# Eighteen of 24 gate tiles made ahead of the attention, as nine pairs in seven block products each

## The chip, the cores and the metric

The kernel runs on one core of a Trainium2 chip. The metric is the time of one execution on the device in microseconds; the profile is of one such execution. TensorE (PE) makes the products, and loads its weights in a stream of its own (PEld); VectorE (DVE), ScalarE (ACT) and GpSimd (POOL) do the elementwise work; SyncE (SP) issues most of the transfers.

## What is computed

One layer of a decoder over 1024 tokens of width 1024, all in float32. The normed input u is multiplied by one wide matrix, and the columns of the result go to three mixers and to their gates:

```
u = rmsnorm(x)
[pool_v | q | k | v | f | z | xBC | dt | gates] = u @ W_in
y_A = pooling(pool_v) @ P_pool
y_B = forgetting_attention(q, k, v, f) @ P_attn
y_C = ssd(z, xBC, dt) @ P_ssd
x = x + (sigmoid(g_A)*y_A + sigmoid(g_B)*y_B + sigmoid(g_C)*y_C) @ W_out
x = x + (silu(c_g) * c_v) @ W_down,   [c_g | c_v] = conv3(rmsnorm(x) @ W_up)
out = rmsnorm(x)
```

The gates are 3 x 1024 columns, in the kernel 24 tiles of 128 columns by 1024 tokens.

## The kernel before

A tile of u @ W_in has its 128 columns on the partitions and the 1024 tokens along the row, in two halves of 512. u lies in SBUF for the whole of this part as a high and a low float32r part, `uh` and `ul`, each in two tiles by halves of the tokens, [128, 8, 512] (8 blocks of 128 of the inner dimension). A weight tile is loaded into `wraw` (one buffer) and split into `whi` (ScalarE, L112) and `wlo` (VectorE, L105), three buffers each. `mm3` (L117) makes each product from three: high by high, high by low, low by high (L123). One gate tile is thus 2 halves x 8 blocks x 3 = 48 products of 128x128 by 128x512.

The work comes in this order in the program: the norm and transposes of x; the f and dt columns; the pooling mixer; the SSD mixer in two passes, one for each group g (`ssd_inputs(g)`: six tiles with a convolution, then the z product; `ssd_chunks(g)`: eight chunks of 128 tokens, one after the other through a state); then `gates()`, the first NGATE1 = 8 gate tiles in PSUM tile `big` (2 buffers of two banks), with the sigmoid; then the v product (`in_proj_tok`: 8 token tiles of 24 products each, weights in the three `whi`/`wlo` buffers and a fourth pair, `xhi`/`xlo`). All of this stands in one SBUF pool, `ssd`, whose tiles follow each other in the order in which the program first names them: acc, BT, CT, xs, xhi, xlo, zs, and then those of the chunks, cbm, xd, yt, xdf, xdh, xdl, bth, btl, mt, state and so on. A pool that is opened after another was closed lies on the same addresses, and each of its tiles waits for the tiles of the old one that it lies on.

Then comes the attention (`attend`, four pairs of heads) with `others(pr)` behind each pair: the q and k products of the next pair and some of the other 16 gate tiles, cut by GCUT into 5, 5, 4 and 2. They are made in halves (PSUM tile `half`, L249) and stored without a sigmoid, which `gate_now` applies when it reads them back for the branches. After the attention follow the three branches (`branch4` and the SSD's), the output product, and the FFN.

The order on each engine isn't the program's: when the kernel is built, a scheduler runs through it with a cost model and puts on each engine what is ready by it, first what stands first in the program. So the first gate tiles, and the gates of `others`, are put into the gaps of the SSD chunks and of the attention.

The FFN up product (L1007 to L1083) already works in pairs of tiles with seven block products in place of eight: the 2 x 2 blocks A11 to A22 of a pair of weight tiles, with sums S1 to S4 of them, are multiplied by blocks of the activations (B11, B21, B22) and by sums T1 to T4 of these. Each such product is 4 blocks x 3 = 12 matmuls. `split_next` splits the next operand into a ring of places ahead of its product.

Of the kernel before, what the change touches and what calls it, by code (L numbers as in the profile page):

```python
# [46 lines left out]
def hybrid_kernel(ctx: ExitStack, tc: tile.TileContext, x, xT, w_in, w_z, w_v, w_fd, mixw, p_pool, p_attn,  # L47
# [33 lines left out]
    def bank():  # L81
        return pst("bank")
# [184 lines left out]

    g_d = dpool.tile([24, P, 1024], F32, name="g_d")

    def gate(i, halves):  # L270

        if halves:
            parts = in_proj_halves(T_GATE + i)
        else:
            ps = in_proj(T_GATE + i)
            parts = [(slice(h * 512, (h + 1) * 512), ps[:, h * 512:(h + 1) * 512]) for h in range(2)]
        for hs, ps in parts:
            gt = gpool.tile([P, 512], F32, name="gt")
            if i < NGATE1:
                nc.scalar.activation(gt, ps, AF.Sigmoid)  # L280
            else:
                nc.scalar.copy(gt, ps)
            nc.sync.dma_start(g_d[i][:, hs], gt)
# [157 lines left out]
    NGATE1 = 8  # L441
    GCUT = (0, 5, 10, 14, 16)
    v_d = dpool.tile([NATT, P, NT, 256], F32, name="v_d")
    yn_d = dpool.tile([NT, P, 1024], F32, name="yn_d")
    with ExitStack() as st:
# [130 lines left out]
        def gates():  # L576
            for i in range(NGATE1):
                gate(i, False)
                yield

# [4 lines left out]
        run(gates())  # L585

        for t, ps in in_proj_tok([w_v[kp, 0] for kp in range(4)], sp):
            vs = sp.tile([P, 8, 2, 64], R32, name="vs", tag="xs", bufs=5)
            pv = ps.rearrange("p (h d) -> p h d", d=64)
            nc.scalar.copy(vs[:, :, 0, :], pv)  # L590
            sub_lo(nc.vector, vs[:, :, 1, :], pv, vs[:, :, 0, :])
            nc.sync.dma_start(v_d[:, :, t, :].rearrange("r p c -> p r c"),
                              vs.bitcast(F32).rearrange("p (r h) x d -> p r (h x d)", h=2))
# [36 lines left out]
    with ExitStack() as st:  # L630
# [120 lines left out]
        def others(pr):  # L751

            todo = range(NGATE1 + GCUT[pr], NGATE1 + GCUT[pr + 1])
            res = None
            if pr + 1 < NATT:
                res = yield from qkv(pr + 1)
            for i in todo:
                gate(i, True)
                yield
            return res  # L760
# [83 lines left out]
    def hl(t):  # L844
        return t[:, 0], t[:, 1]

    HL = [P, 2, 4, 512]
    LO, HI = slice(0, 512), slice(512, 1024)
    B11, B21, B22 = [hl(slot(i, HL, R32, n)) for i, n in enumerate(("b11", "b21", "b22"))]

    with ExitStack() as st:
# [77 lines left out]
        def up_load(n):  # L929

            if n < FT:
                q = 2 * ((n + 1) % 2)
                for x in range(2):
                    nc.sync.dma_start(ab[:, q + x, :], f_up[2 * ORDER[n] + x])

        for j in range(5):
            w = load_w(w_out[j])
            if j == 1:
                for i in range(2):
                    nc.sync.dma_start(ab[:, i, :], f_up[2 * i])  # L940
                up_load(0)
            for h in range(2):
                run(out_tile(j, h, w))
# [12 lines left out]

# [3 lines left out]
        LATE, ALL = ("S1", "S2", "S4", "S3"), ("A11", "S1", "S2", "A12", "S4", "S3")  # L960
        ring, parts = [], {}
        todo = []
        for n in range(FT + 1):
            names = [(n, name) for name in (() if n == FT else LATE if ORDER[n] < NPRE else ALL)]
            if n > 0:
                names.insert(names.index((n, "S2")) if names else 0, (n - 1, "A22"))
            todo += names
        n_split = [0]
        s12, s34 = None, ss

        def up_block(n, name):
            if name[0] == "S":
                t, c = (s12, s34)[(int(name[1]) - 1) // 2], (LO, HI)[(int(name[1]) - 1) % 2]
                return t[:, c]
            return ab[:, 2 * ((n + 1) % 2) + int(name[1]) - 1, (LO, HI)[int(name[2]) - 1]]

        SUMS = {"S1": ("A21", "A22", ALU.add), "S2": ("S1", "A11", ALU.subtract), "S3": ("A11", "A21", ALU.subtract),
                "S4": ("A12", "S2", ALU.subtract)}

        def up_sum(n, *names):  # L980

            if n < FT:
                for name in names:
                    x, y, op = SUMS[name]
                    nc.vector.tensor_tensor(up_block(n, name), up_block(n, x), up_block(n, y), op=op)

        def split_next():

            if n_split[0] == len(todo):
                return  # L990
            n, name = todo[n_split[0]]
            hi, lo = ring[n_split[0] % len(ring)]
            n_split[0] += 1
            src = up_block(n, name)
            nc.scalar.copy(hi, src)
            sub_lo(nc.vector, lo, src, hi)
            parts[n, name] = hi, lo
            if name == "A22":
                up_load(n + 2)
            if name == "S2":  # L1000
                if n == 0:
                    up_load(1)
                up_sum(n + 1, "S1", "S2")
            if name == "S3":
                up_sum(n + 1, "S4", "S3")

        def prod(ps, n, name, b, first=True):  # L1007

            w = parts[n, name]
            for k in range(4):  # L1010
                c = slice(k * P, (k + 1) * P)
                m = mm3([ps], (w[0][:, c], w[1][:, c]), [(b[0][:, k, :], b[1][:, k, :])], first and k == 0, k == 3,
                        skip_group_check=not first)
            split_next()
            return m

        def conv_act(i, ca, cb):

            v, g = [sp.tile([P, 1024], F32, name="vg", bufs=2) for _ in range(2)]
            for t, c, acc in ((2 * i + 1, cb, v), (2 * i, ca, g)):  # L1020
                w = [vec[:, V_FW + 3 * t + k:V_FW + 3 * t + k + 1] for k in range(3)]
                nc.scalar.activation(acc, c, AF.Identity, bias=vec[:, V_FB + t:V_FB + t + 1], scale=w[2])  # L1022
                for s in (1, 2):
                    nc.vector.scalar_tensor_tensor(out=acc[:, s:], in0=c[:, 0:1024 - s], scalar=w[2 - s],  # L1024
                                                   in1=acc[:, s:], op0=ALU.mult, op1=ALU.add)
            nc.scalar.activation(g, g, AF.Silu)
            nc.vector.tensor_tensor(g, g, v, op=ALU.mult)
            nc.sync.dma_start(act_d[i], g)
# [21 lines left out]
        def pair(n, c, last):  # L1050


            i = ORDER[n]
            ca, cb = c
            chain, b5 = bank(), bank()
            if i < NPRE:
                for x, t in ((0, cb[:, LO]), (1, ca[:, LO])):
                    nc.sync.dma_start(t, pre_d[i, x])
            else:
                prod(chain, n, "A11", B11)  # L1060
                nc.scalar.copy(ca[:, LO], chain)
            prod(b5, n, "S1", T1)
            nc.scalar.copy(cb[:, HI], b5)
            if last is not None:
                fourth(n - 1, *last)
            prod(chain, n, "S2", T2, first=i < NPRE)
            if i < NPRE:
                nc.tensor.matmul(chain, lhsT=ident, rhs=cb[:, LO], start=False, stop=True, skip_group_check=True)  # L1068
            nc.scalar.copy(ca[:, HI], chain)
            if i >= NPRE:  # L1070
                b2 = bank()
                prod(b2, n, "A12", B21)
                nc.vector.tensor_tensor(ca[:, LO], ca[:, LO], b2, op=ALU.add)
            prod(b5, n, "S4", B22, first=False)
            nc.vector.tensor_tensor(ca[:, HI], ca[:, HI], b5, op=ALU.add)
            prod(chain, n, "S3", T3, first=False)
            nc.vector.tensor_tensor(cb[:, HI], cb[:, HI], chain, op=ALU.add)
            return chain, c

        def fourth(n, chain, c):  # L1080
            prod(chain, n, "A22", T4, first=False)
            nc.scalar.copy(c[1][:, LO], chain)
            conv_act(ORDER[n], *c)  # L1083

# [4 lines left out]
        for i in range(NPRE + 1):  # L1089
# [14 lines left out]
            if i == 2:  # L1104
                s12 = wpool.tile([P, 1024], F32, name="wraw", bufs=WRAW)
                up_sum(0, "S1", "S2", "S4", "S3")
# [4 lines left out]
        for _ in range(3):  # L1111
            hi, lo = [wpool.tile([P, 1024], R32, name=n, bufs=WHL) for n in ("whi", "wlo")]
            ring += [(hi[:, c], lo[:, c]) for c in (LO, HI)]
        ring += [(more[:, 0, r, :], more[:, 1, r, :]) for r in range(4)]
        for _ in range(len(ring)):
            split_next()
        last = None
        for i in range(FT):
            last = pair(i, (cc[:, 2 * (i % 2)], cc[:, 2 * (i % 2) + 1]), last)
# [208 lines left out]
```

## Time and profile before

| | |
|---|---|
| median of 3 runs | 1877.65 us (1876.23 to 1878.08) |
| the profiled execution | 1876.14 us, span 1874.4 us |
| granted TensorE clock, mean | 0.995 |
| busy: PE, DVE, ACT, POOL | 98%, 58%, 46%, 8% of the span |

The page of the profile gives the busy time of each engine, the span in 40 equal slices (a digit is the busy share of a slice in tenths), the chain of waits that ended last, the costliest groups of instructions and the transfers. The time of a single matmul in it includes its pipeline overlap with the next; the distance of starts is what TensorE needs for one.

### The profile page before, as it was taken

What the parts mean: (1) busy time and instruction counts of PE and PEld (TensorE: products, weight loads), DVE (VectorE), ACT (ScalarE), POOL (GpSimd) and SP (SyncE); (2) the same over time, 40 slices, a digit from 0 to 9 for tenths busy, and PEclk for the clock granted to TensorE, in tenths of its full rate; (3) what the DMA queues carried; (4) which work ended last, traced back from release to release, by engine and by line L of the source; (5) the groups of instructions that cost most, each with busy time, mean ns of one, the idle gap of its engine ahead of it and who ended that gap; (6) DMA issues with size and microseconds to landing.
All of it is one profiled execution on the core that took longest, in us unless ns stands there. A gap on an engine that the chain in (4) does not pass through costs nothing.

```text
span 1874.4 us, 22365 instructions
## 1 busy us (share of the span) xinstructions
PE 1841.7 (98%) x8622; PEld 1504.7 (80%) x8622; DVE 1086.6 (58%) x1611; ACT 856.8 (46%) x1384; POOL 157.1 (8%) x119
## 2 busy tenths in 40 slices
PE   7999999999999999999999999999999999999997
PEld 6888888888878778787788888878888888888886
DVE  6752682661265553655765432878787887743424
ACT  5343584573255463654633322545454555533221
POOL 0100240330000000000022002320000000000000
PEclk9999999999999999999999999999999999999998
DMA  4231231333511313124364451443333321664532
GB/s 153 84 120 34 85 108 57 101 130 104 175 65 62 107 51 129 40 90 153 121 200 135 145 180 68 152 135 124 102 107 118 104 91 53 214 235 157 180 102 68
DMA packets 81629, 217.35 MB, mean 116 GB/s; under 512 B 8625, under 2 KB 15217, under 8 KB 80754
## 3 DMA queue, kind: packets, MB, share of 16 engines
q1 hardware_dynamic: 76192, 201.82, 31.9%
q0 software_dynamic: 1728, 8.39, 1.4%
q10 hardware_dynamic: 3602, 5.72, 0.9%
q8 instruction: 67, 1.10, 0.2%
q14 instruction: 40, 0.33, 0.1%
HBM read 164.41 MB, written 51.48 MB: 115 GB/s over the span
## 4 chain that ended last, share of the span: by engine, by line
PE 93%; DVE 2%; DMA 2%; ACT 1%; issue 1%; POOL 0%; SPq 0%; DVEq 0%; ACTq 0%; POOLq 0%
PE p_bank L123 40%; PE p_big L123 19%; PE p_half L123 17%; PE p_bank L265 2%; PE p_bank L264 2%; PE p_bank L263 2%; PE p_po L722 2%; PE p_sc L674 2%; PE p_pt L697 2%; PE p_bank L557 1%; PE p_sc L673 1%; PE p_bank L1068 0%; DMA yi<-yn_d 0%; PE p_bank L324 0%; DMA ab<-in_f_up_dram 0%
## 5 line engine op out<-in xcount | busy, mean ns | idle before, releaser
L105 DVE TENSOR_TENSOR wlo<-wraw,whi 128x1024 fp32r<-128x1024 f32 (+1 forms) x109 | 126.3, 1159 | 162.8 <-ACT whi L112 161.3
L123 PE MATMUL p_bank<-act,whi 128*128 128x512 f32 (+1 forms) x736 | 218.5, 381 | 0.0
L123 PE MATMUL p_big<-uh,whi 128*128 128x512 f32 (+1 forms) x416 | 157.4, 379 | 0.5 <-ACT whi L112 0.5
L123 PE MATMUL p_big<-uh,wlo 128*128 128x512 f32 (+1 forms) x416 | 157.2, 378 | 0.5 <-DVE wlo L105 0.5
L123 PEld LDWEIGHTS p_bank<-act,whi 128*128 128x128 f32 x736 | 136.0, 188 | 26.6
L123 PE MATMUL p_big<-ul,whi 128*128 128x512 f32 (+1 forms) x416 | 156.7, 377 | 0.0
L123 PE MATMUL p_half<-uh,whi 128*128 128x512 f32 x384 | 153.4, 399 | 0.0
L123 PE MATMUL p_half<-ul,whi 128*128 128x512 f32 x384 | 153.0, 399 | 0.0
L123 PE MATMUL p_half<-uh,wlo 128*128 128x512 f32 x384 | 152.2, 397 | 0.0
L112 ACT CAST whi<-wraw 128x1024 fp32r<-128x1024 f32 x81 | 84.9, 1048 | 137.6 <-PE p_big L123 68.4
L123 PE MATMUL p_bank<-act,wlo 128*128 128x512 f32 (+1 forms) x368 | 139.2, 381 | 0.0
L123 PE MATMUL p_bank<-t,whi 128*128 128x512 f32 x440 | 137.2, 391 | 0.0
L123 PE MATMUL p_bank<-b,whi 128*128 128x512 f32 x376 | 118.9, 397 | 2.2 <-ACT whi L1046 2.0
L1024 DVE SCALAR_TENSOR_TENSOR vg<-cc,vec,vg 128x1023 f32<-128x1023 f32 (+1 forms) x88 | 110.3, 1278 | 8.4 <-ACT vg L1022 8.3
L105 DVE TENSOR_TENSOR wlo<-stage,whi 128x1024 fp32r<-128x1024 f32 x44 | 54.1, 1230 | 101.2 <-ACT whi L112 101.0
L112 ACT CAST whi<-stage 128x1024 fp32r<-128x1024 f32 x44 | 46.1, 1051 | 115.2 <-PE p_bank L123 106.7
L123 PEld LDWEIGHTS p_bank<-t,whi 128*128 128x128 f32 x440 | 82.6, 188 | 17.8
L123 PE MATMUL p_bank<-t,ring 128*128 128x512 f32 x396 | 96.4, 391 | 0.0
L172 POOL TENSOR_TENSOR ss<-ss,vg 128x512 f32<-128x512 f32 (+1 forms) x21 | 30.0, 1429 | 763.7 <-ACT vg L171 763.5
L123 PEld LDWEIGHTS p_big<-uh,wlo 128*128 128x128 f32 x416 | 78.9, 190 | 14.6 <-DVE wlo L105 0.8
L123 PEld LDWEIGHTS p_big<-uh,whi 128*128 128x128 f32 x416 | 79.0, 190 | 14.2 <-ACT whi L112 0.9
L123 PEld LDWEIGHTS p_big<-ul,whi 128*128 128x128 f32 x416 | 79.0, 190 | 13.5
(307 smaller groups left out, 4067.7 us busy)
## 6 DMA issues: line engine op xcount, KB each, us to landing
ab<-in_f_up_dram SPq DMA_DIRECT2D x53, 512.0 KB, 3.3
wraw<-in_w_in_dram SPq DMA_DIRECT2D x48, 512.0 KB, 3.4
stage<-in_f_down_dram SPq DMA_DIRECT2D x44, 512.0 KB, 3.5
g_d<-gt SPq DMA_DIRECT2D x48, 256.0 KB, 2.0
gt<-g_d SPq DMA_DIRECT2D x48, 256.0 KB, 3.4
act_d<-vg SPq DMA_DIRECT2D x22, 512.0 KB, 3.0
stage<-act_d SPq DMA_DIRECT2D x22, 512.0 KB, 4.5
mt<-acs_d SPq DMA_DIRECT2D x16, 512.0 KB, 4.4
```

Of the source, the lines that this page charges most:

```text
L105: eng.tensor_tensor(lo, src, hi.bitcast(F32), op=ALU.subtract)
L112: nc.scalar.copy(hi, raw)
L123: m = nc.tensor.matmul(o, lhsT=wt, rhs=ah[part], start=first and i == 0, stop=last and i == 2, **kw)
L172: eng.tensor_tensor(ss, ss, sq, op=ALU.add)
L263: nc.tensor.matmul(ps, lhsT=a, rhs=hi[:, c], start=k == 0, stop=False)
L264: nc.tensor.matmul(ps, lhsT=a, rhs=lo[:, c], start=False, stop=False)
L265: nc.tensor.matmul(ps, lhsT=ul[t // 4][:, k, q], rhs=hi[:, c], start=False, stop=k == NT - 1)
L557: nc.tensor.matmul(py[:, d], lhsT=mt[:, h * P:(h + 1) * P], rhs=xd[:, d], start=True, stop=True)
L674: nc.tensor.matmul(pss[:, 0:w], lhsT=Q2[h][hp, qs], rhs=KL[hp, j0:j0 + w], start=False, stop=True)
L697: nc.tensor.transpose(pt[:, off + (i - qq[0]) * P:off + (i - qq[0] + 1) * P], in_=probs[i][:, kb * P:(kb + 1) * P], identity=ident)
L722: nc.tensor.matmul(po[:, q0:q0 + w], lhsT=VV[:, kb, h, :], rhs=t[:, o:o + w], start=pc == 0 and i == 0, stop=last and i == len(prods) - 1)
L1024: nc.vector.scalar_tensor_tensor(out=acc[:, s:], in0=c[:, 0:1024 - s], scalar=w[2 - s], in1=acc[:, s:], op0=ALU.mult, op1=ALU.add)
```

## The change

The block products of the FFN become a class, `BlockProduct`, which takes the order of the pairs, the source of the weights, the blocks of the activations and what is done with a finished pair. The FFN uses it as before. A second use makes gate tiles 0 to 17 in nine pairs, behind the SSD passes and ahead of the attention, with the weight ring in the three `whi`/`wlo` buffers (six places). The blocks B11, B21 and B22 are slices of `uh` and `ul`; T1 to T4 are made by `t_sums` in four 16 KB tiles in a new pool `t`, which is opened after `ssd` is closed. The v product moves behind a change of the PSUM pools (eight buffers of one bank, in place of `big` and `bank`), into a pool `v` behind `t`, with steps of `t_sums` between its token tiles; the v results get two buffers (they had five). The weights of the pairs (`ab`), the sums S3 and S4 and the results (`cc`) lie in a pool `gp`, opened when `v` is closed. The sigmoid is applied when a pair is done, and the four halves are stored. In the attention GCUT leaves 2, 2, 1 and 1 gate tiles.

```diff
+    class BlockProduct:
+        LATE, ALL = ("S1", "S2", "S4", "S3"), ("A11", "S1", "S2", "A12", "S4", "S3")
+        SUMS = {"S1": ("A21", "A22", ALU.add), "S2": ("S1", "A11", ALU.subtract),
+                "S3": ("A11", "A21", ALU.subtract), "S4": ("A12", "S2", ALU.subtract)}
...
+        def load(self, n):
+            if n < len(self.order):
+                for x in range(2):
+                    nc.sync.dma_start(self.ab[:, 2 * ((n + 1) % 2) + x, :], self.src(self.order[n], x))
...
+        def prod(self, ps, n, name, b, first=True):
+
+            w, b = self.parts[n, name], self.blocks[b]
+            for k in range(4):
+                c = slice(k * P, (k + 1) * P)
+                mm3([ps], (w[0][:, c], w[1][:, c]), [(b[0][:, k, :], b[1][:, k, :])], first and k == 0, k == 3,
+                    skip_group_check=not first)
+            self.split_next()
+
+        def pair(self, n, c, last):
...
+                self.prod(chain, n, "A11", "B11")
+                nc.scalar.copy(ca[:, LO], chain)
+            self.prod(b5, n, "S1", "T1")
+            nc.scalar.copy(cb[:, HI], b5)
+            if last is not None:
+                self.fourth(n - 1, *last)
+            self.prod(chain, n, "S2", "T2", first=is_early)
...
+            nc.scalar.copy(ca[:, HI], chain)
+            if not is_early:
+                b2 = bank()
+                self.prod(b2, n, "A12", "B21")
+                nc.vector.tensor_tensor(ca[:, LO], ca[:, LO], b2, op=ALU.add)
+            self.prod(b5, n, "S4", "B22", first=False)
+            nc.vector.tensor_tensor(ca[:, HI], ca[:, HI], b5, op=ALU.add)
+            self.prod(chain, n, "S3", "T3", first=False)
+            nc.vector.tensor_tensor(cb[:, HI], cb[:, HI], chain, op=ALU.add)
+            return chain, c
+
+        def fourth(self, n, chain, c):
+            self.prod(chain, n, "A22", "T4", first=False)
+            nc.scalar.copy(c[1][:, LO], chain)
+            self.done(self.order[n], *c)
...
-    NGATE1 = 8
-    GCUT = (0, 5, 10, 14, 16)
+
+    NGATE1 = 18
+    GCUT = (0, 2, 4, 5, 6)
...
-        run(gates())
-
-        for t, ps in in_proj_tok([w_v[kp, 0] for kp in range(4)], sp):
-            vs = sp.tile([P, 8, 2, 64], R32, name="vs", tag="xs", bufs=5)
...
+    psum(bank=(512, 8))
+    with ExitStack() as st:
+        tp = pool("t", stack=st)
+        blocks = {n: (uh[h][:, ks, :], ul[h][:, ks, :])
+                  for n, h, ks in (("B11", 0, slice(0, 4)), ("B21", 0, slice(4, 8)), ("B22", 1, slice(4, 8)))}
+        blocks.update({n: hl(tp.tile(HL, R32, name=n)) for n in ("T1", "T2", "T3", "T4")})
+
+        def t_sums(sp):
+
+            for k in (0, 2):
+                f = {}
+                for n, h, k0 in (("T1", 0, k), ("T3", 1, k), ("T2", 1, k + 4), ("T4", 0, k + 4)):
+                    ks = slice(k0, k0 + 2)
+                    f[n] = sp.tile([P, 2, 512], F32, name=f"f{n}", bufs=1)
+                    nc.vector.tensor_tensor(f[n], uh[h][:, ks, :].bitcast(F32), ul[h][:, ks, :].bitcast(F32),
+                                            op=ALU.add)
+                    if n != "T2":
+                        yield
+                for n, x, y in (("T1", "T3", "T1"), ("T3", "T2", "T3"), ("T2", "T2", "T1"), ("T4", "T4", "T2")):
+                    nc.vector.tensor_tensor(f[n], f[x], f[y], op=ALU.subtract)
+                    hi, lo = blocks[n]
+                    ks = slice(k, k + 2)
+                    nc.scalar.copy(hi[:, ks, :], f[n])
+                    sub_lo(nc.vector, lo[:, ks, :], f[n], hi[:, ks, :])
+                    yield
+
+
+        with ExitStack() as st2:
+            sp = pool("v", bufs=2, stack=st2)
+            ts = t_sums(sp)
+            next(ts)
+            for t, ps in in_proj_tok([w_v[kp, 0] for kp in range(4)], sp):
+                vs = sp.tile([P, 8, 2, 64], R32, name="vs")
...
+                next(ts, None)
+                next(ts, None)
+            for _ in ts:
+                pass
+        sp = pool("gp", stack=st)
+
+        def gates_done(i, ca, cb):
+            for x, c in enumerate((ca, cb)):
+                for hs in (LO, HI):
+                    gt = gpool.tile([P, 512], F32, name="gt")
+                    nc.scalar.activation(gt, c[:, hs], AF.Sigmoid)
+                    nc.sync.dma_start(g_d[2 * i + x][:, hs], gt)
+
+        gp = BlockProduct(list(range(NGATE1 // 2)), lambda i, x: w_in[T_GATE + 2 * i + x], blocks,
+                          sp.tile([P, 4, 1024], F32, name="ab"), gates_done)
+        gp.s12, gp.s34 = wpool.tile([P, 1024], F32, name="wraw", bufs=WRAW), sp.tile([P, 1024], F32, name="s34")
+        gp.load(0)
+        gp.sums(0, "S1", "S2", "S4", "S3")
+        gp.run(w_ring(), sp.tile([P, 4, 1024], F32, name="cc"))
```

## Rows read from the trace of the kernel before

**Rows 1.** The page: busy us, share, instructions; TensorE's busy tenths in 40 slices.

```profile
PE 1841.7 (98%) x8622; PEld 1504.7 (80%) x8622; DVE 1086.6 (58%) x1611; ACT 856.8 (46%) x1384; POOL 157.1 (8%) x119
...
PE   7999999999999999999999999999999999999997
```

**Rows 2.** The page: the chain of waits that ended last, shares by engine.

```profile
PE 93%; DVE 2%; DMA 2%; ACT 1%; issue 1%; POOL 0%; SPq 0%; DVEq 0%; ACTq 0%; POOLq 0%
```

**Rows 3.** The same chain in order of time: start us, us, what, count.

```profile
144.72 10.88 PE p_big L123 x48
...
1411.38 32.94 PE p_bank L123 x144
```

**Rows 4.** Stretches: us; PE, PEld, DVE, ACT, POOL busy; clock, DMA share, GB/s.

```profile
204.00:282.00 78.00, 78.00 (x430) 67.20 (x427) 67.22 (x91) 61.54 (x124) 32.19 (x25) 1.00 0.33 112
338.00:421.50 83.50, 82.39 (x451) 70.05 (x450) 58.92 (x86) 57.37 (x118) 33.06 (x25) 1.00 0.38 128
421.50:501.20 79.70, 79.70 (x353) 65.95 (x353) 14.70 (x21) 19.37 (x27) 1.08 (x1) 1.00 0.33 111
501.20:957.00 455.80, 451.74 (x2162) 354.50 (x2160) 257.18 (x496) 236.10 (x434) 6.55 (x12) 1.00 0.31 103
1243.00:1513.00 270.00, 270.00 (x1166) 218.65 (x1165) 216.02 (x280) 139.29 (x199) 0.00 (x0) 1.00 0.32 109
```

**Rows 5.** Groups of instructions, 338 to 421.5: busy us, mean ns, idle before.

```profile
L123 PE MATMUL p_big<-uh,wlo 128*128 128x512 f32 x75 | 30.1, 401 | 0.0
...
L105 POOL TENSOR_TENSOR xdl<-xdf,xdh 128x512 fp32r<-128x512 f32 x7 | 11.0, 1577 | 72.3 <-ACT xdh L508 72.3
...
L105 DVE TENSOR_TENSOR wlo<-wraw,whi 128x1024 fp32r<-128x1024 f32 x6 | 7.6, 1259 | 1.9 <-ACT whi L112 1.7
...
L280 ACT ACT_TABLE_LOAD x4 | 5.1, 1283 | 0.1
```

**Rows 6.** The chain in order of time, second SSD pass, 385 to 425.

```profile
389.63 1.73 PE p_bank L557 x16
...
393.53 0.32 SPq L283
...
393.94 4.59 DMA mt<-acs_d
...
398.56 2.16 ACT mt L522 x7
...
414.81 1.28 ACT L523
...
416.11 1.07 ACT mt L523
...
417.20 1.23 DVE mt L525
```

**Rows 7.** Groups by shape in the attention, 501.2 to 957, VectorE and ScalarE.

```profile
L105 DVE TENSOR_TENSOR wlo<-wraw,whi 128x1024 fp32r<-128x1024 f32 x29 | 35.5, 1223 | 30.6 <-ACT whi L112 30.6
L105 DVE TENSOR_TENSOR pl<-p_pt,ph 128x512 fp32r<-128x512 f32 x48 | 32.5, 684 | 15.1 <-ACT ph L702 15.0
...
L702 ACT CAST ph<-p_pt 128x512 fp32r<-128x512 f32 x48 | 27.6, 584 | 19.6 <-PE p_pt L697 18.7
```

**Rows 8.** The page: transfers, count, KB each, median us to landing.

```profile
ab<-in_f_up_dram SPq DMA_DIRECT2D x53, 512.0 KB, 3.3
...
g_d<-gt SPq DMA_DIRECT2D x48, 256.0 KB, 2.0
```

**Rows 9.** Stretches with waits on TensorE, columns as in rows 4.

```profile
880.00:890.00 10.00, 8.62 (x40) 6.09 (x40) 7.31 (x15) 6.44 (x12) 2.13 (x4) 0.93 0.99 330
890.00:900.00 10.00, 10.00 (x51) 8.00 (x51) 7.64 (x15) 5.37 (x11) 0.00 (x0) 0.90 0.39 143
900.00:910.00 10.00, 7.32 (x45) 5.75 (x46) 8.85 (x22) 9.49 (x21) 0.00 (x0) 1.00 0.32 105
1865.00:1874.00 9.00, 1.03 (x4) 0.29 (x2) 4.63 (x15) 0.20 (x1) 0.00 (x0) 0.50 0.35 117
```

More of the change, by code (lines that the diff above doesn't have):

```diff
@@ L278, in gate, with w_ring @@
+    def w_ring():
+        ring = []
+        for _ in range(WHL):
+            hi, lo = [wpool.tile([P, 1024], R32, name=n, bufs=WHL) for n in ("whi", "wlo")]
+            ring += [(hi[:, c], lo[:, c]) for c in (LO, HI)]
+        return ring
+    g_d = dpool.tile([24, P, 1024], F32, name="g_d")
+    def gate(i):
+        for hs, ps in in_proj_halves(T_GATE + i):
             gt = gpool.tile([P, 512], F32, name="gt")
[L279 to L282, printed above, removed]
+            nc.scalar.copy(gt, ps)
@@ L757, in others @@
             for i in todo:
-                gate(i, True)
+                gate(i)
                 yield
@@ L927, in hybrid_kernel, with conv_act, early_results @@
         ab = slot(3, [P, 4, 1024], F32, "ab")
[L929 to L934, printed above, removed]
+        def conv_act(i, ca, cb):
+            v, g = [sp.tile([P, 1024], F32, name="vg", bufs=2) for _ in range(2)]
+            for t, c, acc in ((2 * i + 1, cb, v), (2 * i, ca, g)):
+                w = [vec[:, V_FW + 3 * t + k:V_FW + 3 * t + k + 1] for k in range(3)]
+                nc.scalar.activation(acc, c, AF.Identity, bias=vec[:, V_FB + t:V_FB + t + 1], scale=w[2])
+                for s in (1, 2):
+                    nc.vector.scalar_tensor_tensor(out=acc[:, s:], in0=c[:, 0:1024 - s], scalar=w[2 - s],
+                                                   in1=acc[:, s:], op0=ALU.mult, op1=ALU.add)
+            nc.scalar.activation(g, g, AF.Silu)
+            nc.vector.tensor_tensor(g, g, v, op=ALU.mult)
+            nc.sync.dma_start(act_d[i], g)
+        def early_results(i, p1, c11):
+            for x, t in ((0, p1), (1, c11)):
+                nc.sync.dma_start(t, pre_d[i, x])
+        up_blocks = {"B11": B11, "B21": B21, "B22": B22}
+        up = BlockProduct(ORDER, lambda i, x: f_up[2 * i + x], up_blocks, ab, conv_act, NPRE, early_results)
+        up.s34 = ss
         for j in range(5):
@@ L1007, in prod @@
[L1007 to L1028, printed above, removed]
+        up_blocks.update(T1=T1, T2=T2, T3=T3, T4=T4)
@@ L1048, in early_w @@
             return hi, lo
[L1050 to L1083, printed above, removed]
         ew = [early_w(i) for i in range(2)]
@@ L1110, in hybrid_kernel @@
         cc = upool.tile([P, 4, 1024], F32, name="cc", tag="ul1")
[L1111 to L1119, printed above, removed]
-        fourth(FT - 1, *last)
+        up.run(w_ring() + [(more[:, 0, r, :], more[:, 1, r, :]) for r in range(4)], cc)
         stage = slot(3, [P, 4, 1024], F32, "stage")
```

129 lines of the change are left out of this document (66 added, 63 removed).

## The prediction, made before the changed kernel was run

> **What bounds the kernel now.** I read the page's busy table and slices first [rows 1]: TensorE is busy 98% of the span, nine tenths or more in every slice but the first and the last, while VectorE has 58% and ScalarE 46%. The chain of waits says the same in another way [rows 2]: 93% of the path to the end is TensorE's own work. So a TensorE instruction taken out of a covered stretch is worth its whole issue time, and any wait that reaches TensorE costs its whole length. The chain in order of time gives that issue time [rows 3]: one gate-sized tile, 48 matmuls of 512 columns back to back, takes 10.88 us, 0.2267 us a matmul. (The mean of one instruction, near 0.4 us, includes its pipeline overlap and is not used.) Then I cut the span where the change cuts the program [rows 4]: the second pass of the SSD chunks (338 to 421.5), the rest of the early gates and the v product (to 501.2), attention with the first branch (to 957), and, as a model of the new stage, the FFN up stage, which already makes block products.
>
> Of the second SSD pass the reader should see that it is not a TensorE stage. TensorE is busy 82.4 of 83.5 us there, but three rows of 75 gate matmuls each stand in it [rows 5]: 225 x 0.2267 = 51.0 us are gate tiles that the compiler has put in the pass's gaps. The pass's own TensorE work is 82.4 - 51.0 = 31.4 us.
>
> **The change part by part.**
>
> *Fewer products.* Two gate tiles cost 96 matmuls now and 7 x 4 x 3 = 84 as a pair. Nine pairs save 108 matmuls: 108 x 0.2267 = **-24.5 us**. That the pairs can run at this rate is shown by the FFN up stage: 144 matmuls in 32.94 us, 0.2288 each with two identity products between the stretches [rows 3]. At that rate nine pairs would cost 9 x 84 x 0.0021 = 1.6 us more, the other end. The work of VectorE and ScalarE for a pair is 14 and 15 operations of 512 columns, 0.684 and 0.584 us [rows 7], so 9.6 and 8.8 us under 19.0 us of products; the FFN stage hides more, VectorE 216 of 270 us busy with TensorE at 270 of 270 [rows 4]. Nothing for it. The four stores and two loads of a pair on SP's queue are 2.0 us and 3.3 us to landing [rows 8], under the same 19 us and two buffers deep; nothing.
>
> *The cover of the second SSD pass goes.* This is the main cost. The eight gates used to fill the pass. Now the next work in program order is the v product, and it stands behind a change of pools. PSUM is no obstacle: four of the eight new banks lie on the old `big`, free by then. SBUF is. The four T tiles are 64 KB a partition and lie exactly on acc, BT, CT, xs, xhi, xlo and zs (4+8+8+20+4+4+16); so the pool `v` begins where cbm, xd, yt, xdf and the rest of the chunk's tiles lie, which live to the last chunk. The fourth pair of weights of the v product, xhi and xlo, comes to lie on xd, yt and xdf. Before the pass ends only the three pairs in the ring can be used: 18 of 24 matmuls of a tile, on four free banks, 72 x 0.2267 = 16.3 us of cover instead of 51.0.
>
> How long is the pass without the gates? Below by VectorE: 58.9 us busy in it [rows 4], less 7.6 us for six gate splits [rows 5], plus three v splits (3.8 us): 55 us. Above by what it takes now, 83.5. It is nearer the lower end, because the chain now goes through the gates [rows 6]: the load of mt waits on SP behind a gate's store (393.53), ScalarE's exponential waits behind a gate's table load, sigmoid and table load back (414.81, with 1.28 us for each load and four of them for gates alone in the pass [rows 5]), and products wait behind gate matmuls in TensorE's order. All that goes. What is left of the loop of one mt buffer is 4.59 us of load, some 2.5 and 1.1 us of ScalarE, 1.23 of VectorE and 1.73 of products: 11.1 us for two chunks, under VectorE's 14. VectorE reached 86% in the first pass [rows 4]; that gives 64 us, all of it 55. I take 59. TensorE then idles 59 - 31.4 - 16.3 = **+11.3 us** (7.3 at 55, 16.3 at 64, 35.8 at 83.5).
>
> *A gap ahead of the first pair.* `ab` lies on xhi, xlo, the f tiles and one vs, so its load can't be issued before the last v matmul; nothing else is ready, since the weight ring belongs to the pairs. Load 3.3 us [rows 8] for the first half tile and as much again, at most, for the second behind it, then a ScalarE and a VectorE operation (1.3 us): 4.6 to 8 us, I take 6.3. Beside it lie the T sums: 24 VectorE operations of 1024 columns (1.22 us each by the weight split's row [rows 7], 29 us), which can't start before the pass ends, plus eight v splits and xlo (6.7 us): 36 us against the 27.2 us of v products that are left (120 matmuls) and the gap. T1 and T2, made first, are in time; the last T may be 2 us late. Together **+7.3 us** (4.6 to 12).
>
> *The clock.* Between 880 and 890 TensorE waits for 1.4 us, and the granted clock is 0.93 and then 0.90 in the next 10 us [rows 9]: (0.07 + 0.10) x 10 = 1.7 us at full speed lost. The gap is longer: **+1.5 us** (0 to 4). The pass, with TensorE 81% busy (47.7 of 59), I leave at nothing: the stretch from 900 is 73% busy at a clock of 1.00 [rows 9]. The Trainium skill (TensorE: Matmul & The Clock Gate, HAM oscillation) speaks against the change here: a kernel that waits between bursts of products falls to the lower level each time and starts each burst there. By that rule the pass too would run at half speed; the trace agrees for a wait with little around it (0.50 in the last 9 us [rows 9]) and not for one inside dense work.
>
> *Attention.* Ten gate tiles leave it; their products are counted above. What they leave behind is less cover: TensorE needs 451.7 - 108.8 = 343 us, VectorE 257.2 - 10 x 1.22 = 245 [rows 4, 7], 71% where it was 56%. VectorE held 80% in the FFN stage and 86% in the first SSD pass with TensorE full [rows 4], and each pair still has the q and k products of the next one and one or two gates. I take **+1 us** (-3 to +12; the upper end is three more stretches like 880 to 910, where TensorE lost 4.06 us [rows 9], one for each pair). Reading gates 8 to 17 without a sigmoid frees ScalarE and moves nothing on TensorE.
>
> Sum: -24.5 + 11.3 + 7.3 + 1.5 + 1 = -3.4 us. The profiled execution took 1876.14 us around its span of 1874.4, so **1872.7, say 1873 us**; the median of the runs shown is 1.5 us above that execution, so this is 0.25% under it. Differences under 0.2% (3.8 us) can't be told from no change here.
>
> **The rivals.**
>
> *The cover holds.* If the compiler gets the v product into the pass in full (43.5 us), 31.4 + 43.5 covers 59 us and the 11.3 are gone; with a gap at its lower end it is 1876.1 - 24.5 + 4.6 + 1.5 + 1 = 1859 us. For it: products of a new stage do run before the old one ends when their space is free. Against it: the map of the tiles above.
>
> *The pass keeps its pace* (the side of slower). If something other than the gates sets 10.4 us a chunk, the load of mt and POOL's 1.6 us operations in the state's chain [rows 5], the pass stays near 83.5 us, idles 35.8, and the time is 1897. For it: VectorE is only 71% busy there [rows 4] and its waits are on ScalarE and on TensorE. Against it: those are the engines which the gates hold up. It turns the sign at a pass of 62.4 us and is a measurable loss from 66.
>
> *Attention starves.* At its upper end, +12 instead of +1: 1884 us. For it: before, the only stretch with the cover used up had the only waits. Against: the sums above.
>
> *The pass runs at the lower clock.* Its products, 47.7 us, would take 95 at half the clock throughout; at half of the pass, 72 us against 59, +13: 1886 us. The rule of the page stands beside this.
>
> **How the numbers follow.** My forecast, a small gain left over, has 0.47; its own range is 1865 to 1880 (pass 51 to 66). The cover holds 0.20, the pass keeps its pace 0.16, attention starves 0.12, the clock 0.05. Faster: 0.20 + 0.27 of the forecast's 0.47, since its middle lies just beyond the bound, 0.47. Within 0.2%: 0.15 of it and 0.05 of the mild ends of the others, 0.20. Slower: the remaining 0.33. The range runs from 1858 to 1893: the covered case is in it, of the pass that keeps its pace only the shorter half.
>
> **What would show it.** 84 matmuls a pair at about 19.0 us from one pair to the next. In the second pass, TensorE at 47 or 48 us busy, no p_half or gate products, the first v matmuls with whi alone and none with xhi before the last chunk. A pass of 55 to 64 us from its first product of C and B to its last py. One wait of 5 to 8 us for `ab` and a lower clock just behind it. Attention at about 343 us with VectorE above 70% and few waits on TensorE. I am wrong if xhi is read inside the pass, if the pass stays over 66 us, if waits of several us stand inside the pairs, or if attention's waits on TensorE come to more than 10 us.

## The result, and the profile after

The changed kernel takes **1931.87 us** (median of 4 runs, 1931.34 to 1935.69) against 1877.01 us for the kernel before on the same chip: ratio **1.0296**, 95% interval 1.0278 to 1.0314, so some 55 us slower. I had forecast 1873 us, a gain too small to be sure of. The prediction was wrong in sign, and 1931.87 lies far outside its range.

The profiled execution took 1931.34 us around a span of 1929.5 us, 55.1 us more than before. Its page, against [rows 1, 2] (busy TensorE; its busy tenths and its granted clock in 40 slices; the chain that ended last):

```profile
PE 1856.2 (96%) x8514; PEld 1512.0 (78%) x8514; DVE 1168.7 (61%) x1743; ACT 881.8 (46%) x1445; POOL 154.7 (8%) x119
...
PE   7999999798999999999889999999999999999997
...
PEclk9999999788999999998799999999999999999999
...
PE 90%; DVE 5%; DMA 3%; ACT 1%; issue 1%; POOL 0%; SPq 0%; DVEq 0%; ACTq 0%
```

The 108 products are gone (8514 matmuls for 8622), and TensorE is nevertheless busy 14.5 us longer: a matmul at a lower clock is a longer busy time. The holes in both rows of digits stand at the same two places, around 340 to 450 us and around 860 to 1010 us. Stretches of the changed kernel, columns as in [rows 4]: the second SSD pass, the v product, the gap, the nine pairs, attention with the first branch, and the second branch with the SSD norm.

```profile
337.30:402.10 64.80, 50.36 (x227) 41.23 (x226) 55.39 (x82) 39.40 (x99) 29.13 (x25) 0.70 0.28 101
402.10:447.00 44.90, 44.87 (x193) 36.66 (x192) 35.03 (x40) 15.40 (x20) 0.00 (x0) 0.97 0.26 88
447.00:454.80 7.80, 0.00 (x0) 0.00 (x1) 0.71 (x2) 1.25 (x3) 0.00 (x0) 0.63 0.72 227
454.80:629.40 174.60, 173.82 (x756) 143.41 (x757) 85.11 (x128) 78.96 (x134) 0.00 (x0) 0.99 0.32 105
...
629.40:997.10 367.70, 352.17 (x1662) 270.65 (x1660) 235.22 (x476) 209.75 (x397) 6.55 (x12) 0.95 0.29 92
997.10:1059.50 62.40, 55.48 (x261) 45.11 (x261) 38.54 (x54) 13.04 (x23) 20.76 (x15) 0.95 0.58 181
```

The last stretch was not in the rows of before; there it is

```profile
957.00:1007.00 50.00, 49.80 (x242) 41.15 (x242) 34.53 (x47) 19.41 (x34) 19.20 (x15) 1.00 0.59 185
```

So the ledger against before, with 10 x 10.88 = 108.8 us for the ten gate tiles that move from attention to the front:

| part | before, gates moved | after | difference | predicted |
|---|---|---|---|---|
| second pass to attention's start | 163.3 + 108.8 = 272.1 | 292.1 | +20.0 | -4.4 |
| attention with the first branch | 455.8 - 108.8 = 347.0 | 367.7 | +20.7 | +1 |
| second branch | 50.0 | 62.4 | +12.4 | 0 |
| the rest | 867.4 | 870.0 | +2.6 | 0 |

The pass begins 0.6 us sooner, which leaves the 55.1 us. Two losses are to be explained, then: 24.4 us more than forecast in front of the attention and 32.1 us more in it and right behind it.

**In front.** Groups of instructions on the v product's weights between 330 and 400 us, then its first product (timeline of TensorE), then the chain around the gap:

```profile
L112 ACT CAST whi<-wraw x3: 1045/1045/1055, 333.4 to 347.6; 128x1024 fp32r<-128x1024 f32 x3
L105 DVE TENSOR_TENSOR wlo<-wraw,whi x3: 1212/1224/1575, 334.5 to 349.5; 128x1024 fp32r<-128x1024 f32 x3
```
```profile
401.89 0.77 PE L263 MATMUL p_bank<-whi,uh 128*128 128x512 f32 x1
```
```profile
447.01 0.59 ACT vs L734
447.62 0.70 DVE vs L105
448.34 0.36 SPq L736
448.93 5.18 DMA ab<-in_w_in_dram
454.13 0.63 ACT whi L320
454.80 5.28 PE p_bank L123 x13
```

Three pairs of weights are split by 351 us, and yet not one v product runs before the pass's last product: the cover that I counted at 16.3 us is nothing. The gap is as I described it, a load that waits for the last v tile's place, 7.8 us for my 6.3.

**In attention.** Stretches of 20 us near its end:

```profile
880.00:900.00 20.00, 17.63 (x96) 13.03 (x94) 16.85 (x40) 13.11 (x29) 0.00 (x0) 0.99 0.09 32
900.00:920.00 20.00, 17.68 (x59) 11.32 (x58) 16.45 (x41) 11.93 (x29) 0.00 (x0) 0.67 0.15 51
920.00:940.00 20.00, 13.20 (x48) 10.33 (x48) 12.77 (x25) 11.01 (x18) 0.00 (x0) 0.57 0.43 132
940.00:960.00 20.00, 20.00 (x102) 15.63 (x102) 15.14 (x31) 10.76 (x21) 0.00 (x0) 1.00 0.26 79
```

From 900 to 940 us TensorE issues 107 products where it issues about 200 in 40 us elsewhere. What was missing beside the attention, by the operations on the gate buffers `gt` (count, ns, first and last start):

```profile
L763 SPq DMA_DIRECT2D gt<-g_d x16: 319/320/320, 930.2 to 989.9; - x16
L784 DVE TENSOR_TENSOR mg<-p_half,gt x16: 673/691/694, 932.9 to 996.3; 128x512 f32<-128x512 f32 x16
L939 SPq DMA_DIRECT2D gt<-o_d x6: 319/320/320, 868.3 to 927.7; - x6
L940 ACT CAST oh<-gt x6: 601/617/619, 916.7 to 930.6; 128x512 fp32r<-128x512 f32 x6
```

The last gate product ends at 869 us. The first branch then fills both `half` banks by 888 us, but its first result can't be multiplied with a gate before 932.9: both gate buffers have gone to reloaded attention results, from 868 on, and these wait for the third head pair to end, on whose tiles `oh` lies. For 45 us attention has nothing beside it. Of the 20.7 us that this stretch lost, 11.5 are waits of TensorE (15.5 us for 4.1) and 9.2 a longer busy time of the same products, at a granted clock of 0.95. Attention ends at 1001.6 us, after the first branch, and the next stage's loads start only then (VectorE's wait, then TensorE's):

```profile
1009.29 1.42 DVE L970 SCALAR_TENSOR_TENSOR yi<-yi,rs_r,snr 128x512 f32<-128x512 f32 x2 [5.58 <-DMA snr<-in_row_dram]
```
```profile
1010.10 1.97 PE L974 MATMUL p_bank<-cst,yi 128*128 128x128 f32 x8 [5.13 <-DVE yi L970]
```

### The profile page after: what moved, and what is told of

Its sections match the earlier page's. It is cut to its first block, busy times and chain, and to the rows that moved or that the text cites. A ratio compares the mean times of both kernels' runs of the same rounds, so it can differ in the third digit from the quotient of the medians.

```text
span 1929.5 us, 22405 instructions
## 1 busy us (share of the span) xinstructions
PE 1856.2 (96%) x8514; PEld 1512.0 (78%) x8514; DVE 1168.7 (61%) x1743; ACT 881.8 (46%) x1445; POOL 154.7 (8%) x119
## 3 DMA queue, kind: packets, MB, share of 16 engines
q1 hardware_dynamic: 76192, 201.82, 31.2%
## 4 chain that ended last, share of the span: by engine, by line
PE 90%; DVE 5%; DMA 3%; ACT 1%; issue 1%; POOL 0%; SPq 0%; DVEq 0%; ACTq 0%
PE p_bank L123 48%; PE p_big L123 15%; PE p_half L123 11%; PE p_bank L263 2%; PE p_bank L265 2%; PE p_bank L264 2%; PE p_po L885 2%; PE p_sc L837 1%; PE p_pt L860 1%; PE p_bank L675 1%; PE p_sc L836 1%; DVE ns L838 1%; PE p_bank L974 0%; PE p_bank L359 0%; DVE mt L643 0%
## 5 line engine op out<-in xcount | busy, mean ns | idle before, releaser
L112 ACT CAST whi<-wraw 128x1024 fp32r<-128x1024 f32 x63 | 66.1, 1049 | 116.5 <-PE p_big L123 70.4
L123 PE MATMUL p_big<-uh,whi 128*128 128x512 f32 (+1 forms) x288 | 107.1, 372 | 0.5 <-ACT whi L112 0.5
L123 PE MATMUL p_big<-uh,wlo 128*128 128x512 f32 (+1 forms) x288 | 106.7, 371 | 0.5 <-DVE wlo L105 0.5
L123 PE MATMUL p_big<-ul,whi 128*128 128x512 f32 (+1 forms) x288 | 106.8, 371 | 0.0
L123 PE MATMUL p_half<-uh,whi 128*128 128x512 f32 x224 | 90.7, 405 | 0.0
L123 PE MATMUL p_half<-ul,whi 128*128 128x512 f32 x224 | 89.9, 401 | 0.0
L123 PE MATMUL p_bank<-T,whi 128*128 128x512 f32 x288 | 88.5, 389 | 0.8 <-DVE cc L368 0.8
L123 PE MATMUL p_half<-uh,wlo 128*128 128x512 f32 x224 | 88.9, 397 | 0.0
L123 PEld LDWEIGHTS p_bank<-b,whi 128*128 128x128 f32 x376 | 71.1, 190 | 21.3 <-ACT whi L1149 3.9
L123 PEld LDWEIGHTS p_bank<-t,ring 128*128 128x128 f32 x396 | 74.3, 188 | 16.3
```

Of the source, the lines that this page charges most:

```text
L112: nc.scalar.copy(hi, raw)
L123: m = nc.tensor.matmul(o, lhsT=wt, rhs=ah[part], start=first and i == 0, stop=last and i == 2, **kw)
```

## Experiments

The theory after the result: attention's loss comes from six gate tiles being too little cover (work that TensorE can do while the stage's own chain waits), the loss in front from the uncovered pass and the gap; the block products themselves do what they should. The rivals: that the pairs leave something behind that attention trips over, or that the fall of the clock is what costs. Each run's time is a median; ratios are to the kernel before on the same chip.

### Attention without block products, and block products without the cut

The kernel before with the new numbers:

```
-    NGATE1 = 8
-    GCUT = (0, 5, 10, 14, 16)
+    NGATE1 = 18
+    GCUT = (0, 2, 4, 5, 6)
```

> The kernel before with 18 plain gate tiles ahead of the attention and 6 in it: no block products, as many matmuls as before. Theory (attention lives on its gate tiles): the 20.9 us that attention lost and the 12.4 us that the second branch lost in the changed kernel come back here whole, so about 1877 + 33 = 1910 us. Rival (the block products leave something behind that attention trips over, such as queues or the place of its tiles): no loss without them, 1874 to 1881 us.

1907.65 us, ratio 1.0157 (1.0142 to 1.0172). And the changed kernel with the old numbers:

```
-    NGATE1 = 18
-    GCUT = (0, 2, 4, 5, 6)
+    NGATE1 = 8
+    GCUT = (0, 5, 10, 14, 16)
```

> The changed kernel with block products for the first 8 gate tiles only (four pairs), so that attention keeps 16 as before. Theory (the losses add up: pass and start of the pairs 44 us, attention and second branch 33 us): 1877 + 44 - 4 x 12 x 0.2267 = 1910 us, with attention at 456 us from its first product to the second branch. Rival (attention's loss does not hang on its number of gates): 1932 + 13.6 us of products no longer saved = 1945 us.

1918.80 us, ratio 1.0221 (1.0204 to 1.0238). Stretches from attention's first product to the second branch and through it, the first kernel, then the second:

```profile
609.70:975.60 365.90, 348.69 (x1661) 267.80 (x1660) 237.28 (x478) 210.12 (x396) 6.56 (x12) 0.97 0.28 94
975.60:1038.00 62.40, 55.15 (x261) 45.23 (x261) 41.19 (x54) 13.04 (x23) 19.84 (x15) 0.95 0.57 181
```
```profile
537.90:994.70 456.80, 451.84 (x2161) 354.14 (x2159) 255.21 (x495) 236.25 (x435) 6.56 (x12) 1.00 0.30 101
994.70:1045.10 50.40, 49.87 (x240) 41.14 (x241) 35.38 (x47) 19.26 (x33) 19.32 (x15) 1.00 0.57 182
```

With six tiles and no block product at all attention loses as in the changed kernel, 365.9 and 62.4 us; with sixteen tiles behind four pairs it loses nothing, 456.8 and 50.4 against 455.8 and 50.0. The theory holds on both sides, and the rival is out. The second run's median is 9 us above the theory's figure; in its profiled execution (span 1913.6 us) the front lost 48 us instead of 44, with a pass of 68.5 us.

### Cover for the pass

```
-    NGATE1 = 18
+    NGATE1, NPLAIN = 18, 4
...
         run(ssd_chunks(1, *a1))
+        for i in range(NPLAIN):
+            ps = in_proj(T_GATE + i)
+            for h in range(2):
+                gt = gpool.tile([P, 512], F32, name="gt")
+                nc.scalar.activation(gt, ps[:, h * 512:(h + 1) * 512], AF.Sigmoid)
+                nc.sync.dma_start(g_d[i][:, h * 512:(h + 1) * 512], gt)
...
-        gp = BlockProduct(list(range(NGATE1 // 2)), ...
+        gp = BlockProduct(list(range(NPLAIN // 2, NGATE1 // 2)), ...
```

> The changed kernel with gate tiles 0 to 3 as plain products that may fill the second SSD pass, and seven pairs for 4 to 17. Theory (the pass is slow because it has no cover and its clock falls): two pairs go (-38.1 us), the pass grows from 64.6 to about 31.4 + 43.5 = 75 us at the full clock: about 1904 us. Rival (the pass is bound by its own chain, and the clock only falls because TensorE waits): the gates fill its 14.4 idle us and add the rest, about 94 us in the pass: 1923 us.

1910.84 us, ratio 1.0178 (1.0163 to 1.0193), 21 us less than the changed kernel although it saves 24 products fewer, and nearer to the theory's 1904 than to the rival's 1923. The pass took 84.1 us at a clock of 0.94, longer than the theory had it and about as long as before [rows 4]; but the gates bring 43.5 us of work into it for 19.3 us of length.

### Does the low clock lengthen the pass?

Products into an unread bank, eight behind each state product, and in the other run sixteen (they compute nothing that is used):

```
+                last = mm3([pns], btm, [xdd])
+                if g == 1:
+                    fill = big()
+                    with tc.issue_after(last):
+                        for k in range(8):
+                            nc.tensor.matmul(fill[:, 0:512], lhsT=uh[0][:, k, 0:P], rhs=uh[0][:, k, :],
+                                             start=k == 0, stop=k == 7)
```

> The changed kernel with 56 products of 128x512 more in the second SSD pass, eight behind each state product, into a bank that nobody reads (12.7 us of TensorE at full clock that compute nothing). Theory (the low clock lengthens the pass): the pass, 64.6 us at a clock of 0.70, gets no longer or shorter, 58 to 64 us at a clock above 0.9: 1925 to 1932 us. Rival (the chain of the other engines sets it and the clock costs nothing): the added products lie in the chain of TensorE and the pass grows by 5 to 13 us: 1937 to 1945 us.

> The changed kernel with 112 products more in the second SSD pass, sixteen behind each state product, that compute nothing (25.4 us of TensorE at full clock, twice the run with eight). Theory (the low clock lengthens the pass, so keeping TensorE busy gives the time back): the clock in the pass is 0.95 or more and the pass is no longer than the 64.8 us without them. Rival (the chain of the other engines sets the pass and the clock costs it nothing; added products stand in the chain): the clock rises all the same, and the pass takes 70 us or more.

1924.03 us, ratio 1.0251 (1.0226 to 1.0275), and 1931.12 us, ratio 1.0283 (1.0261 to 1.0304). The pass, from its first product to its last, in those two:

```profile
338.03:405.46 67.43, 57.14 (x281) 47.23 (x280) 53.78 (x80) 38.73 (x97) 30.12 (x24) 0.82 0.27 92
```
```profile
338.52:408.34 69.82, 62.45 (x339) 53.31 (x338) 52.34 (x82) 39.31 (x98) 29.48 (x25) 0.93 0.26 89
```

In the kernels whose pass is that of the changed one it took 64.8 us at a clock of 0.73 (the run with later gates, below) to 68.5 us at 0.67 (the run with four pairs). So the filler raises the clock to 0.82 and 0.93; 12.7 us of it cost nothing beyond that spread and 25.4 us cost 1 to 5 us; and the pass gets no shorter. Keeping TensorE busy does not give time back here. Of its forecasts for the pass the first run met neither; the second ends on the rival's side. What the low clock itself costs the pass is not settled by this, because the filler stands in the way of what it speeds up. From the chain that ends last, in the changed kernel, then in the run with sixteen:

```profile
376.54 2.16 PE p_bank L675 x16
...
398.46 3.67 PE p_bank L675 x16
```
```profile
364.03 3.65 PE p_big L666 x16
367.68 1.73 PE p_bank L681 x16
```

Four such rows of 16 products stand in the changed kernel's chain, 11.0 us in all, and one takes 1.73 us in the kernel before [rows 6]: some 4 us lie in these rows alone. Against that the filler (L666) stands in the chain with 9.0 us in the first run and 15.0 us in the second, so a gain by the clock and the price of the filler can cancel. The first run's median is 8 us under the changed kernel, its profiled execution only 0.7 us (span 1928.8); there the pass and the front are longer, and attention with the second branch shorter (424.0 us for 430.1), so the pass is not where it gains.

### Accumulators for the v product

```
-            ps = bank()
+            ps = big()[:, 0:512] if wide else bank()
...
-    psum(bank=(512, 8))
...
-            for t, ps in in_proj_tok([w_v[kp, 0] for kp in range(4)], sp):
+            for t, ps in in_proj_tok([w_v[kp, 0] for kp in range(4)], sp, True):
...
+        psum(bank=(512, 8))
         sp = pool("gp", stack=st)
```

> The changed kernel with the accumulators of the v product on the two wide PSUM tiles, which the pass does not use, and the change to eight banks behind that product. Theory (the v product stayed out of the second SSD pass for want of a free accumulator, not of weights): two token tiles with 18 products each run inside the pass, the rest behind it, 36 x 0.2267 = 8.2 us less between the end of the pass and the first pair: 1922 to 1926 us. Rival (they only lie in the way of the pass's own chain): the pass grows by as much as they take, 1930 to 1936 us.

1935.40 us, ratio 1.0321 (1.0291 to 1.0351). TensorE's waits from 395 to 480 us:

```profile
PE p_big L263 <- ACT xhi L112: 6.9, 1, 6.9
PE p_big L264 <- DVE xlo L105: 4.3, 1, 4.3
```

Now 36 v products run inside the pass, from 338.1 us on, and the pass (67.8 us) stays within the 64.8 to 68.5 us that it takes without them: that much was only want of an accumulator. But nothing is won; the time is in the rival's range, though not by the rival's way. Behind the pass the fourth pair of weights, which lies on the chunk's tiles, is late by 11.2 us, which the changed kernel hides under the other tokens' products, and from the pass's start to attention it takes 303.5 us for 292.1.

### The gap

```
-        gp = BlockProduct(..., sp.tile([P, 4, 1024], F32, name="ab"), gates_done)
...
-        gp.load(0)
+        abp = pool("gab", side="right", stack=st)
+        gp = BlockProduct(..., [None, abp.tile([P, 2, 1024], F32, name="ab1")], gates_done)
+        gp.load(0)
         def t_sums(sp):
...
+        gp.ab[0] = sp.tile([P, 2, 1024], F32, name="ab0")
```

> The changed kernel with the first pair's two weight tiles at a place that is free when the second SSD pass ends, so that they are loaded while the v product runs. Theory (the gap of 7.8 us ahead of the pairs is the load, and the lower clock around it follows from it): the gap is 0 to 2 us and the pairs start at the full clock, 1920 to 1925 us. Rival (VectorE is late with the sums of the activations, and the load was only the last of two): 4 us or more of the gap stay, 1926 to 1931 us.

1917.17 us, ratio 1.0212 (1.0197 to 1.0227), 14.7 us less than the changed kernel. Where the gap was, 446 to 456 us:

```profile
446.00:456.00 10.00, 10.00 (x46) 8.29 (x45) 4.92 (x9) 4.25 (x9) 0.00 (x0) 1.00 0.61 206
```

The gap is gone and the clock stays up; VectorE's sums were in time. Counted from the pass's start, attention starts 9.3 us sooner, and the second branch takes 4.6 us less, for which I have no cause.

### Where the six tiles stand, and the gate buffers

```
-    GCUT = (0, 2, 4, 5, 6)
+    GCUT = (0, 1, 2, 4, 6)
```

> The changed kernel with the same six gate tiles in attention, handed out 1, 1, 2, 2 over the four head pairs instead of 2, 2, 1, 1. Theory (the six are used up by 869 us, and what lacks is cover at the end): two more tiles of 10.9 us behind that point, 1910 to 1922 us. Rival (six tiles are too few wherever they stand; the waits only move ahead): 1927 to 1938 us, with waits before 820 us.

1931.05 us, ratio 1.0288 (1.0273 to 1.0304). And, without that,

```
-                t = gpool.tile([P, 512], F32, name="gt")
+                t = sp.tile([P, 512], F32, name="ot2", bufs=1)
                 nc.sync.dma_start(t, o_d[k][:, hs])
```

> The changed kernel with a buffer of its own for the reloads of the attention's results, which held the two gate buffers from 868 to 931 us. Theory (between 888 and 933 us the first branch's products stood still because no gate tile could be loaded, and that stretch is where attention lost its cover): the first product with a gate is by 885 us instead of 933, TensorE waits and falls in clock less between 880 and 1000: 1905 to 1918 us. Rival (attention's own chain sets its end whatever lies beside it; the cover is only used sooner): 1926 to 1934 us, the end of attention still near 1000 us.

1926.68 us, ratio 1.0251 (1.0226 to 1.0277). In the second, the first gate multiplication and the stretches:

```profile
L784 DVE TENSOR_TENSOR mg<-p_half,gt x16: 679/690/692, 891.5 to 952.4; 128x512 f32<-128x512 f32 x16
```
```profile
900.00:920.00 20.00, 20.00 (x104) 16.27 (x103) 14.51 (x31) 9.29 (x21) 0.00 (x0) 1.00 0.39 120
920.00:940.00 20.00, 20.00 (x92) 14.26 (x93) 15.95 (x35) 10.10 (x21) 0.00 (x0) 1.00 0.37 122
...
960.00:980.00 20.00, 16.88 (x67) 11.90 (x66) 16.40 (x36) 13.60 (x27) 0.00 (x0) 0.67 0.08 27
980.00:1000.00 20.00, 16.94 (x92) 13.78 (x91) 15.57 (x44) 16.21 (x42) 0.00 (x0) 0.90 0.00 0
```

The branch runs 41 us sooner and TensorE is full where it starved, but then the branch is over at 952 us and attention starves behind it. The time falls into the rival's range: the cover was spent sooner. Later gates change nothing in the time, as their rival said, and TensorE waits sooner (6.5 us between 620 and 820 us, 2.5 in the changed kernel). So the held buffers say where the hole is, not that there is one.

### How many tiles are enough

The changed kernel with six plain tiles ahead (as in the cover run), four pairs, `GCUT = (0, 3, 6, 8, 10)` and the early load; then the same with the change to eight banks behind the v product (as in the accumulator run) and the first weight tile of the second branch ahead of the norm; then that with an own buffer; and that with five pairs and `GCUT = (0, 2, 4, 6, 8)`.

```
+        branch4(1, p_attn, oh, ol, sp, False, range(1))
         for g in range(2):
             snr = sp.tile([P, 512], F32, name="snr", bufs=1)
...
-        branch4(1, p_attn, oh, ol, sp, False)
+        branch4(1, p_attn, oh, ol, sp, False, range(1, 4))
```

> Six gate tiles as plain products that may fill the second SSD pass, four pairs for the next eight, ten gate tiles in attention, and the early load of the first pair. Theory (pass, gap and attention each keep their cover, so that the saved products show): 4 x 12 x 0.2267 = 10.9 us less than before, up to 4 us for what is left of the start: 1867 to 1871 us. Rival (ten tiles leave attention short as well, by a part of the 30 us that it loses with six): 1880 to 1890 us.

> The mixture of six plain gate tiles, four pairs and ten gate tiles in attention, with two waits taken out: the change to eight banks behind the v product (3.3 us at its start), and the first weight tile of the second branch ahead of the SSD output's norm, whose loads start when attention is over (3.5 us on TensorE and a lower clock). Theory (those two waits are what eats the 10.9 us of saved products): 1866 to 1871 us. Rival (the waits come back at the next place, such as the norm's end): 1875 to 1880 us.

> The mixture with ten gate tiles in attention, both waits out, and besides a buffer of its own for the reloads of the attention's results. Theory (between 860 and 900 us TensorE still waits and falls in clock because the first branch has no gate buffer): 3 to 5 us less than the mixture without it, 1868 to 1870 us. Rival (the cover is only used sooner and lacks behind it): 1872 to 1876 us.

> The same with a fifth pair, eight gate tiles in attention, and a buffer of its own for the reloads of the attention's results. Theory (eight tiles still cover attention once the first branch is not held up): 2.7 us under the mixture with ten, 1863 to 1869 us. Rival (attention loses cover between ten and six tiles, in step with their number, some 15 of the 30 us): 1878 to 1886 us.

| gate tiles in attention | kernel | us | ratio, interval | attention and second branch, us over what is due (505.8 as before, less 10.88 for each tile under 16) |
|---|---|---|---|---|
| 16 | four pairs | 1918.80 | 1.0221 (1.0204 to 1.0238) | +1.4 |
| 10 | six plain, four pairs | 1878.17 | 1.0006 (0.9996 to 1.0016) | +5.1 |
| 10 | and both waits out | 1873.24 | 0.9981 (0.9972 to 0.9991) | +3.8 |
| 10 | and an own buffer | 1873.39 | 0.9982 (0.9972 to 0.9992) | +1.4 |
| 8 | five pairs, the same | 1876.25 | 0.9993 (0.9983 to 1.0002) | +9.9 |
| 6 | own buffer alone | 1926.68 | 1.0251 (1.0226 to 1.0277) | +24.4 |
| 6 | no pairs | 1907.65 | 1.0157 (1.0142 to 1.0172) | +31.3 |
| 6 | changed kernel | 1931.87 | 1.0296 (1.0278 to 1.0314) | +33.1 |

The last column is read from one profiled execution each, and it is coarse: in the runs that leave the changed kernel's attention as it is (the cover, filler, gap and accumulator runs) it lies between +23.2 and +31.2, so a gain by the own buffer (+24.4) is not shown by it. The 30 us between sixteen and six tiles stand far above that.

Attention itself keeps its pace with ten tiles, 388.3 us where 390.5 are due; what is lost there is lost behind it. Two stretches of the first mixture:

```profile
562.60:950.90 388.30, 384.56 (x1857) 299.25 (x1855) 242.38 (x482) 217.85 (x412) 5.82 (x11) 1.00 0.28 94
950.90:1008.20 57.30, 53.85 (x256) 43.72 (x257) 38.92 (x52) 15.18 (x26) 19.67 (x15) 0.97 0.63 197
```

At 1878.17 us it lies between theory and rival. With both waits out it is 1873.24 us, again between the two, and 0.19% under the kernel before: with the own-buffer run the best of the study, and hardly more than can be told from no change. With the own buffer attention and the second branch are 2.4 us shorter, the stages behind 2.5 us longer, and the time is the rival's; the run with eight tiles met neither forecast and is no better than ten.

## Why the prediction was wrong

**Fewer products: right.** 756 matmuls for nine pairs, 84 each, in 174.6 us. That is 0.231 us a matmul, 1.6 us above my other end for them, with the start of the pairs behind the gap in it.

**"Attention: +1 us" is the step that failed most.** I compared sums: TensorE 343 us against VectorE 245, 71%. The sums were right, VectorE was even at 64% (235.2 of 367.7), and they were the wrong test. Cover is used in the order in which it comes free: the plain tiles were spent by 869 us, the first branch was stuck or, with its own buffer, spent by 952, and the chain of the last head pairs then ran alone. The rival "attention starves" had the mechanism at +12 us with 0.12; it was +20.7, and +12.4 in the second branch, which I had not counted at all: before, its first loads ran under the end of the first branch. That the block products have no part in it is shown by the run without them (29.8 us over before).

**The pass: "PSUM is no obstacle" failed.** Predicted 59 us with 16.3 us of v products in it; measured 64.8, the top of my range, and none. Free accumulators bring half of them into the pass, and with the two of that run the wait for the weights that I had seen to lie on the chunk's tiles takes it back; whether more accumulators would have paid is open. TensorE idles 14.4 us there for my 11.3, but the pass's own products, 31.4 us in my sum, keep it busy for 50.4 at a granted clock of 0.70, and the v product costs 44.9 behind it for my 27.2. Giving gates back to the pass was worth 21 us. Of the rivals here, "the cover holds" and "the pass keeps its pace" (83.5 us) did not come.

**The gap: right.** Place, load and length came as said, 7.8 for 6.3 us; no T sum was late. Taking it out brought attention 9.3 us forward, and I had 8.8 for the gap and the clock behind it. The run gained 14.7 us; the rest is mostly in the second branch, and its cause is open.

**The clock: the fall in the pass was missed.** I carried one 10 us stretch at 73% busy and clock 1.00 [rows 9] over to the whole pass. The pass is 78% busy, in waits of at most 2.2 us, and the granted clock is 0.70, that is, the lower of the two levels for more than half of it. The rival with this in it had a chance of 0.05. The Trainium skill (TensorE: Matmul & The Clock Gate, A second HAM failure mode: psum-queue depth-cycling) tells of a kernel that cycles through PSUM banks, in which TensorE idles briefly and often between groups of products, goes back and forth between the levels and loses throughput by it. The trace agrees with the first half. Whether the pass lost time by it no run here shows by itself: at 0.82 and 0.93 it was not shorter, but with the filler in its chain. What the clock cost in attention was not tried by itself either.

Behind all this 2.6 us in the FFN stages and the reason why the compiler, in the changed kernel, uses none of the banks that are free during the pass remain open.

## What to carry to other kernels

Work that an engine-bound kernel could do anywhere is often what keeps its dependent stages covered: before moving it, take it out of the order alone, without the new method, and time that. A share of busy time over a whole stage does not show whether cover is left at its end; look which filler is still unissued when the last chain starts, and what the next stage preloads under it. And new space for a stage that should fill an old one must be free in each resource, accumulators and every operand, while the old one still runs.

## What was new about the hardware

The granted clock fell over stretches that had no long wait: it was 0.70 over a pass whose longest wait was 2.2 us, and 0.67 and 0.57 from 900 to 940 us with none above 3.4. In the pass 56 and 112 idle-filling products raised it to 0.82 and 0.93. And a higher clock bought that way was worth nothing: with them the pass took 67.4 and 69.8 us instead of 64.8 to 68.5, 9.0 and 15.0 us of the filling being in its chain. What the low clock costs by itself remains open.
